# A decoder trunk whose queries and keys are projected turned and rotated there, on one core of a Trainium2 chip

## The chip, the cores and the metric

The kernel runs on one core of one Trainium2 chip. The core has a matrix engine, TensorE (PE), which multiplies a standing operand (the weights of the array, loaded ahead of each matmul) with a moving one and adds into PSUM banks of 128 partitions x 512 floats; a VectorE (DVE), a ScalarE (ACT) and a GpSimd (POOL) for the elementwise work; and DMA queues, here those that SyncE (SP) issues. Each engine works through its own instructions in order and waits for the others on semaphores. The metric is the device time of one execution in microseconds. Before the change it is 1394.22 us, the median of three runs (1393.64 to 1394.62).

## What is computed

Two layers of a decoder trunk over 512 tokens of width 1024, in float32. Each layer normalises `x`, projects it once to 2844 columns, and splits these into three groups of heads of 64 channels: forgetting attention (4 heads), sparse attention (8 query heads over 2 groups of keys and values, in a compressed, a selected and a window branch) and dilated attention (4 heads). The heads' outputs go through one output projection; then follows a gated MLP with a short convolution. The queries and keys of the sparse and the dilated heads are rotated in their first 16 channels:

```python
proj = h @ w_in
(fq, fk, fv, ff, nq, kc, vc, ks, vs, kw, vw, ng, dq, dk, dv) = jnp.split(proj, splits, axis=-1)
def partial_rope(x, cos, sin):          # half = 8, ROPE_DIM = 16 of 64 channels
    x1 = x[..., :half]
    x2 = x[..., half:ROPE_DIM]
    return jnp.concatenate([x1 * cos - x2 * sin, x2 * cos + x1 * sin, x[..., ROPE_DIM:]], axis=-1)
o_fox = fox_attention(heads(fq, 4), heads(fk, 4), heads(fv, 4), log_f)
o_nsa = nsa_attention(rope(nq, 8), rope(kc, 2), heads(vc, 2), rope(ks, 2), heads(vs, 2),
                      rope(kw, 2), heads(vw, 2), gates, ...)
o_dil = dilated_attention(rope(dq, 4), rope(dk, 4), heads(dv, 4))
x = x + rms_norm(concat(o_fox, o_nsa, o_dil) @ w_out, attn_post_norm)
x = x + rms_norm(conv_ffn(rms_norm(x, ffn_pre_norm)), ffn_post_norm)
```

With 512 tokens the selected branch has all 8 blocks selected and the window covers the whole sequence, so both are full causal attention over their own keys and values.

## The kernel before

Every operand of a large product is kept as two parts, a high and a low one, whose sum is the float32 number; a product is three matmuls (high x high, high x low, low x high). The weights come by DMA into `raw` tiles, one chunk at a time in the order of a plan; `part_weights` (L136) makes the high part on ACT (L145) and the low one on POOL (L149) or DVE (L153), chunk names in `ONPOOL` taking POOL.

The normalised tokens are kept turned, channels on partitions: `HH(k)` and `HL(k)` are the two parts of channel tile k, [128 channels, 512 tokens]. The scores need queries and keys in that layout too, 64 channels of a head on partitions and tokens along the columns; values are needed the other way, tokens on partitions.

- The projection of most columns is `proj256` (L675): 128 tokens of `HH` or `HL` stand in the array and 256 columns of weights move through it (`s_mms`, L431). The result has tokens on partitions. It takes two PSUM banks `acc` and eight steps of 12 matmuls. The names of the weight chunks are those of the columns: `kc` compressed keys and values, `ks` selected keys and values, `nq0`, `nq1` sparse queries, `kw` window keys and values, `dq`, `dk`, `dv` dilated ones; `fk`, `fv`, `fq` belong to the forgetting heads.
- `staged` (L689) says what follows for queries and keys. Per token tile `rope` (L439) rotates on DVE: three multiplies from PSUM (L442 to L444) and an add (L446) into a row tile `r`, where ACT copies the other channels (L447). Keys get each head twice side by side. Then `turn` (L709) makes four PE transposes (L712) into a bank of the group `pt`, which it shares with the attention, and `keep` parts the bank: `q_evac` (L455; ACT L459, DVE L460) makes a query's high and low part on the two halves of the partitions, `k_evac` (L464; ACT L466, DVE L467) the two parts of a key tile.
- The compressed keys and values go by `kc_evac` and `win`, with transposes at L757; the forgetting keys by `t_block` (L449), with an ACT copy that doubles them (L510) and transposes at L452. The forgetting queries (`fq_proj`) and the MLP (`up_mms`) have the weights standing and the tokens moving already.

PE's order is written by hand; that of DVE, ACT and POOL is left to a scheduler. A unit is a head, a branch and a tile of 128 queries: 16 units of the forgetting heads, 64 of the sparse ones, 16 of the dilated ones. Each slot of a loop sends several units through stages, some slots apart (`LAGS`): scores (`s<-k,q`), row maximum (L1073, DVE), exponential (ACT L1078), norm (POOL L1085), transposes (PE L1096, into `pt`), parting (ACT L1113, DVE L1118), values (`o<-ph,v`). Between the stages the loop takes steps of the other work, the pieces: `RATE` says how many per slot (1.4 in the first twelve, then 0.8); `later(d, fn)` puts a function off by d steps; and `until` takes steps at once as long as a unit's query or key isn't there (in `operands`, L1029 and L1040). `merge` mixes two pieces of a projection with one of `hidden`, the first product of the compression (`acc<-wh_w,wth`).

Of the kernel before, what the change touches and what calls it, by code (L numbers as in the profile page):

```python
# [24 lines left out]
NST = 4  # L25
# [4 lines left out]
ONPOOL = ("dv", "dq", "dk", "ks", "nq0", "kw", "kc", "nq1",  # L30
# [8 lines left out]
TT = "pt"  # L39
# [34 lines left out]
def tile_hybrid_block(  # L74
# [87 lines left out]
    for l in range(DEPTH):  # L162
# [7 lines left out]
        cols("fk", C_FK, spare=True)  # L170
        for c, (k0, k1) in enumerate(((0, 3), (3, 6), (6, 8))):
            plan.append(((l, "fv", c), [(wi[:, k0:k1, C_FV:C_FV + 260], 0, 0), (wi[:, k0:k1, C_NG:C_NG + 24], 0, 260)],
                         k1 - k0, 284, False))
        for c in range(2):
            plan.append(((l, "fq", c), [(wi[:, :, C_FQ + 128 * c:C_FQ + 128 * c + 128], 0, 0)], 8, 128, False))
        cols("kc", C_KC)
        cols("ks", C_KC + 256)
        cols("nq0", C_NQ)
        for kv, (name, c0) in enumerate((("kw", C_KW), ("nq1", C_NQ + 256))):
            for c in range(2):  # L180
                plan.append(((l, name, c), [(wi[:, 4 * c:4 * c + 4, c0:c0 + 256], 0, 0)], 4, 256, False))
# [4 lines left out]
        cols("dq", C_DQ)  # L186
        cols("dk", C_DK)
# [13 lines left out]
    def getw(*key, ahead=AHEAD, pre=None, peek=False):  # L201
        """the parts of a chunk; has those up to `ahead` after it loaded and those up to `pre` after it parted"""
# [21 lines left out]
    def table(func, after):  # L224
        """has the function's table loaded once `after` is there"""
# [20 lines left out]
    # gains of the pre norms, a channel to a partition: they are applied to the turned rows  # L246
# [8 lines left out]
    def turn_pair(half, i, l, tags, tilewise=False):  # L255
        """two token tiles of h, turned over, times the gains, in two parts"""
# [160 lines left out]
    cc = const.tile([128, NST, 16], F32, name="cc")  # L417
    ss = const.tile([128, NST, 16], F32, name="ss")
    nc.scalar.activation(ss[:, :, 8:16], ang, AF.Sin)
    nc.vector.tensor_mul(sinh, sinh, sinh)  # L420
    for o in (0, 8):
        nc.vector.tensor_scalar(cc[:, :, o:o + 8], sinh, -2.0, 1.0, op0=ALU.mult, op1=ALU.add)
    nc.vector.tensor_scalar(ss[:, :, 0:8], ss[:, :, 8:16], -1.0, None, op0=ALU.mult)

    for l in range(DEPTH):
        # ================= mixer =================
# [12 lines left out]
        def rope(dst, src, s, nh):  # L439
            t1 = small.tile([128, nh, 16], F32, tag="rope", bufs=4, name=nm("rope"))  # L440
            t2 = small.tile([128, nh, 16], F32, tag="rope", bufs=4, name=nm("rope"))
            nc.vector.tensor_mul(t1, src[:, :, 0:16], bc(cc[:, s], 1, nh))  # L442
            nc.vector.tensor_mul(t2[:, :, 0:8], src[:, :, 8:16], bc(ss[:, s, 0:8], 1, nh))
            nc.vector.tensor_mul(t2[:, :, 8:16], src[:, :, 0:8], bc(ss[:, s, 8:16], 1, nh))  # L444
# [4 lines left out]
        def t_block(tiles, c0):  # L449
            p = ps("pt")  # L450
            for s in range(NST):
                nc.tensor.transpose(p[:, 128 * s:128 * s + 128], tiles[s][:, c0:c0 + 128], ident)  # L452
            return p
# [235 lines left out]
        def staged(key, turned, dup, nh, v=None, plain=0):  # L689
# [3 lines left out]
            def evac(s, p):  # L693
# [9 lines left out]
                if v is not None:  # L703
                    if s == 0:
                        store[v] = new_v()
# [635 lines left out]
```

## Time and profile before

| | |
|---|---|
| median of three runs | 1394.22 us |
| profiled execution, span of the records | 1390.7 us |
| granted TensorE clock, mean over the span | 0.997 |
| busy: PE, DVE, ACT, POOL | 97%, 63%, 52%, 22% of the span |
| instructions: PE, DVE, ACT, POOL | 8019, 2022, 1541, 363 |

The span goes from the first to the last instruction of the profiled execution; some 3.5 us of the time lie outside it. In the rows below, a group is a line of the kernel with an engine, an operation and tiles (`out<-in`), its count, its busy time and the mean of one; behind the second bar stands the idle time of the engine just before these instructions and what ended it. In a timeline the idle time ahead of an instruction stands in brackets with its releaser. Matmuls overlap in the pipeline, so their pitch is read from their starts, not their durations. The attention of the first layer lies between 72 and 340 us, that of the second between some 740 and 1020 us.

### The profile page before, as it was taken

To read this page: it belongs to the slowest core of one execution; us is meant where nothing else is said; L and a number is where in the kernel's file an instruction comes from. 1 tells how busy PE (TensorE), PEld (TensorE's weight loads), DVE (VectorE), ACT (ScalarE), POOL (GpSimd) and SP (SyncE) were. 2 spreads that over 40 slices of the span, in tenths; PEclk is the share of its full clock that TensorE was granted. 3 is DMA by queue.
4 is the path that set the end of the run, shared out by engine and by line. 5 is a ranking of instruction groups with operands and counts; after the bars stand their busy time and mean duration, and the time that the engine had idled before them with its cause. 6 is when DMAs were issued, how large, how long until landed. Compare 5 with 4: busy or idle time off the path is not lost.

```text
span 1390.7 us, 21646 instructions
## 1 busy us (share of the span) xinstructions
PE 1343.5 (97%) x8019; PEld 1186.6 (85%) x8019; DVE 873.2 (63%) x2022; ACT 728.1 (52%) x1541; POOL 311.5 (22%) x363
## 2 busy tenths in 40 slices
PE   6999999999999999999999999999989999999997
PEld 6899999987888888888899899999878888888886
DVE  6678778678655555433464887876767555554334
ACT  6567767775443333422465677677755333333222
POOL 1363663345000000000004646633430000000000
PEclk9999999999999999999999999999999999999999
DMA  5223311132233333223323142112313333332231
GB/s 178 77 62 110 108 47 41 50 111 74 75 93 93 104 92 102 96 91 121 118 85 107 47 126 88 32 47 62 107 61 101 97 91 106 92 100 97 91 121 61
DMA packets 145521, 123.78 MB, mean 89 GB/s; under 512 B 8264, under 2 KB 135688, under 8 KB 145416
## 3 DMA queue, kind: packets, MB, share of 16 engines
q1 hardware_dynamic: 145416, 122.40, 29.1%
q8 instruction: 63, 1.03, 0.3%
q14 instruction: 42, 0.34, 0.1%
HBM read 118.19 MB, written 4.19 MB: 88 GB/s over the span
## 4 chain that ended last, share of the span: by engine, by line
PE 79%; DVE 11%; ACT 5%; issue 2%; POOL 1%; DMA 1%; SPq 0%; DVEq 0%; ACTq 0%; POOLq 0%
PE acc L114 35%; PE s L114 17%; PE pt L114 13%; PE o L114 10%; PE pt L1096 3%; DVE wt L771 1%; DVE r L1073 1%; DVE hl L267 1%; DVE x L301 1%; DVE r L446 1%; ACT r L1078 1%; ACT r L281 1%; DMA raw_fv<-in_w_in_dram 1%; DVE pl L1118 1%; ACT hh L266 0%
## 5 line engine op out<-in xcount | busy, mean ns | idle before, releaser
L153 DVE TENSOR_TENSOR wl_up<-raw_up,wh_up 128x1024 fp32r<-128x1024 f32 x78 | 95.5, 1225 | 163.2 <-ACT wh_up L145 163.2
L145 ACT ACTIVATE wh_up<-raw_up 128x1024 fp32r<-128x1024 f32 (+1 forms) x90 | 89.6, 1002 | 156.2 <-PE acc L114 68.2
L153 DVE TENSOR_TENSOR wl_wd<-raw_wd,wh_wd 128x1024 fp32r<-128x1024 f32 x42 | 51.5, 1225 | 133.6 <-ACT wh_wd L145 133.6
L1078 ACT ACTIVATE r<-r,sm 128x128 f32<-128x128 f32 x192 | 107.0, 558 | 25.6 <-DVE sm L1073 22.7
L145 ACT ACTIVATE wh_wd<-raw_wd 128x1024 fp32r<-128x1024 f32 x42 | 44.5, 1060 | 144.9 <-PE pt L114 135.6
L1085 POOL TENSOR_SCALAR r<-r,sm,gates 128x128 f32<-128x128 f32 (+3 forms) x128 | 84.1, 662 | 118.6 <-DVE sm L1083 95.9
L149 POOL TENSOR_TENSOR wl_kc<-raw_kc,wh_kc 128x512 fp32r<-128x512 f32 x8 | 11.3, 1426 | 419.7 <-ACT wh_kc L145 419.7
L114 PE MATMUL acc<-hl,wh_up 128*128 128x512 f32 (+1 forms) x272 | 102.6, 377 | 0.0
L114 PE MATMUL acc<-hh,wh_up 128*128 128x512 f32 (+1 forms) x272 | 102.6, 377 | 0.0
L114 PE MATMUL acc<-hh,wl_up 128*128 128x512 f32 (+1 forms) x272 | 102.5, 377 | 0.0
L114 PE MATMUL s<-k,q 128*128 128x512 f32 (+3 forms) x384 | 98.8, 338 | 2.3 <-DVE k L467 1.0
L1118 DVE TENSOR_TENSOR pl<-pt,ph 128x384 fp32r<-128x384 f32 x144 | 85.5, 594 | 10.2 <-ACT ph L1113 9.1
L1073 DVE CUSTOM_DVE_ANT_0 r<-s,cmask 128x128 f32<-128x128 f32 (+3 forms) x160 | 75.5, 482 | 19.3 <-PE s L114 13.8
L1113 ACT ACTIVATE ph<-pt 128x384 fp32r<-128x384 f32 x144 | 75.3, 523 | 21.3 <-PE pt L1096 19.5
L1096 PE MATMUL pt<-ident,r 128*128 128x128 f32 x480 | 77.2, 275 | 6.8 <-DVE pl L1118 3.3
L114 PE MATMUL acc<-wh_wd,gh 128*128 128x512 f32 x252 | 83.8, 389 | 0.0
L114 PE MATMUL s<-hh,wh_up 128*128 128x512 f32 (+1 forms) x224 | 80.7, 360 | 0.4 <-DVE hl L267 0.4
L114 PE MATMUL s<-hl,wh_up 128*128 128x512 f32 (+1 forms) x224 | 80.4, 359 | 0.0
L114 PE MATMUL s<-hh,wl_up 128*128 128x512 f32 (+1 forms) x224 | 80.4, 359 | 0.0
L1265 ACT ACTIVATE r<-r 128x512 f32<-128x512 f32 x44 | 27.8, 632 | 81.3 <-DVE r L1246 81.0
L114 PE MATMUL o<-ph,v 128*128 128x256 f32 (+1 forms) x288 | 69.6, 270 | 0.4 <-DVE mx L1154 0.4
L114 PE MATMUL o<-pl,v 128*128 128x256 f32 (+1 forms) x288 | 67.2, 282 | 1.9 <-DVE pl L1118 1.7
(431 smaller groups left out, 4227.7 us busy)
## 6 DMA issues: line engine op xcount, KB each, us to landing
raw_up<-in_w_up_dram SPq DMA_DIRECT2D x88, 512.0 KB, 3.8
raw_wd<-in_w_down_dram SPq DMA_DIRECT2D x44, 512.0 KB, 3.5
raw_wo<-in_w_out_dram SPq DMA_DIRECT2D x16, 512.0 KB, 3.5
x<-in_x_dram SPq DMA_DIRECT2D x8, 512.0 KB, 6.7
raw_nq<-in_w_in_dram SPq DMA_DIRECT2D x8, 512.0 KB, 3.8
raw_w<-in_cmp_w_k_dram SPq DMA_DIRECT2D x8, 512.0 KB, 3.7
raw_w<-in_cmp_w_v_dram SPq DMA_DIRECT2D x8, 512.0 KB, 3.7
raw_fk<-in_w_in_dram SPq DMA_DIRECT2D x4, 512.0 KB, 7.1
```

Of the source, the lines that this page charges most:

```text
L114: nc.tensor.matmul(o, lhsT=lhsT, rhs=rhs, start=start, stop=stop, skip_group_check=True)
L145: nc.scalar.activation(hi[:, ks], raw[:, ks], AF.Copy)
L153: nc.vector.tensor_sub(lo[:, ks], raw[:, ks], f(hi)[:, ks])
L267: nc.vector.scalar_tensor_tensor(lo, src, gain[:, k:k + 1], f(hi), op0=ALU.mult, op1=ALU.subtract)
L281: nc.scalar.activation(scr, y, AF.Square, accum_out=stats["p", s // 2][:, c:c + 1])
L1073: nc.vector.tensor_tensor_reduce(row[:, 0:n], u["S"][:, 0:n], u["mask"][:, 512 - n:512], op0=ALU.add, op1=ALU.min, scale=1.0, scalar=3.0e3 ...
L1078: nc.scalar.activation(row[:, 0:n], row[:, 0:n], AF.Exp, scale=-1.0, bias=sm_[:, 0:1], accum_out=sm_[:, 1:2])
L1085: nc.gpsimd.tensor_scalar(row[:, 0:n], row[:, 0:n], sm_[:, 2:3], g_, op0=ALU.mult, op1=ALU.mult)
L1096: nc.tensor.transpose(p[:, 128 * b:128 * b + 128], src, ident)
L1113: nc.scalar.activation(hi, src, AF.Copy)
L1118: nc.vector.tensor_sub(*u["lo"])
L1265: nc.scalar.activation(cd[0], cd[0], AF.Silu)
```

## The change

The weight chunks of all queries and keys become 128 columns of all eight channel tiles (`turned`), and the new `projT` has them standing and all 512 tokens moving: 24 matmuls of 512 columns a chunk, in four steps, into one bank. The result is turned already: two heads of 64 channels on the partitions, tokens along the columns. `rope(p)` rotates such a block whole with two tables [128, 512], `cosT` and `sinT`, that hold 1 and 0 in the channels that aren't rotated: a shuffle of partitions on DVE brings each channel's partner, DVE multiplies the block by `cosT`, POOL the shuffled one by `sinT`, and POOL adds them. The tables are built once, by 8 transposes. `q_evac` and `k_evac` read the rotated row tile; `k_evac` makes both heads of a block, each doubled over the partitions. The forgetting keys (no rotation) go from PSUM to `k_evac` straight. The values of the selected and the window branch are one chunk `sv` of 256 columns in the old layout, between `ks` and `nq0`; a unit of these heads asks for it by `until("sv")`. `dv` and `fv` stay. The transposes at L452, L712 and L757 are gone.

```diff
-        def rope(dst, src, s, nh):
...
-            for d in dst:
-                nc.vector.tensor_add(d[:, :, 0:16], t1, t2)
-                nc.scalar.activation(d[:, :, 16:64], src[:, :, 16:64], AF.Copy)
+        def t_mms(p, w, sl, first, last, ks=range(KT)):
+            hi, lo = w
+            for k in ks:
+                mm(p[:, sl], hi[:, k, :], HH(k)[:, sl], first and k == 0, False)
+                mm(p[:, sl], hi[:, k, :], HL(k)[:, sl], False, False)
+                mm(p[:, sl], lo[:, k, :], HH(k)[:, sl], False, last and k == KT - 1)
+        def rope(p):
+            w, r = rt(), rt()
+            nc.vector.stream_shuffle(w, p, PARTNER)
+            nc.vector.tensor_mul(r, p, cosT)
+            nc.gpsimd.tensor_mul(w, w, sinT)
+            nc.gpsimd.tensor_add(r, r, w)
+            return r
...
         def k_evac(p):
-            k = bt([128, 2, 512], F32R, "k")
-            nc.scalar.activation(k[:, 0, :], p, AF.Copy)
-            nc.vector.tensor_sub(k[:, 1, :], p, f(k[:, 0, :]))
-            return k
+            ks = []
+            for j in range(2):
+                k = bt([128, 2, 512], F32R, "k")
+                src = p[64 * j:64 * j + 64, :]
+                for u in (j, 1 - j):
+                    nc.scalar.activation(k[64 * u:64 * u + 64, 0, :], src, AF.Copy)
+                for u in (j, 1 - j):
+                    nc.vector.tensor_sub(k[64 * u:64 * u + 64, 1, :], src, f(k[64 * j:64 * j + 64, 0, :]))
+                ks.append(k)
+            return ks
...
-        store["fk"] = [k_evac(t_block(tl, 128 * j)) for j in range(4)]
+        store["fk"] = k_evac(pk_[0]) + k_evac(pk_[1])
...
-        def staged(key, turned, dup, nh, v=None, plain=0):
...
+        def projT(name, key=None, turn=None):
+            for c in range(sum(z[0:2] == (l, name) for z in where)):
+                w = getw(l, name, c, pre=PRE)
+                p = ps("acc")
+                for k in range(0, KT, 2):
+                    t_mms(p, w, slice(0, 512), True, True, (k, k + 1))
+                    if k == KT - 2:
+                        pieces.later(EV[0], turn[c] if turn else keep, *((p,) if turn else (p, key)))
+                    yield
+        def keep(p, key):
+            pieces.later(EV[3], keep2, rope(p), key)
+        def keep2(r, key):
+            store.setdefault(key, []).extend([q_evac(r)] if key[-1] == "q" else k_evac(r))
...
-            yield from proj256("kc", kc_evac, [(pos_turn,), (win, 0)])
-            pieces.later(3 + 4 * WGAP, win, 1)
-            yield from proj256("ks", *staged("nks", True, True, 2, "vs"))
-            yield from proj256("nq0", *staged("nq", True, False, 4))
+            pieces.later(3, pos_turn)
+            yield from projT("kc", turn=(win_k, win_v))
+            yield from projT("ks", "nks")
+            yield from proj256("sv", sv_evac, [])
+            yield from projT("nq0", "nq")
...
-            for kv, g in ((0, proj256("kw", *staged("nkw", True, True, 2, "vw"))),
-                          (1, proj256("nq1", *staged("nq", True, False, 4)))):
+            for kv, g in ((0, projT("kw", "nkw")), (1, projT("nq1", "nq"))):
...
-            yield from proj256("dq", *staged("dq", True, False, 4))
-            yield from proj256("dk", *staged("dk", True, True, 4))
+            yield from projT("dq", "dq")
+            yield from projT("dk", "dk")
```

Where this moves instructions, in the first layer. On PE, at the first score product over the window keys (`s<-k,q`), before: the end of a part of `hidden` (`acc<-..w_1_0..`) stands between the two turns of the window keys, `pt_1919` for the first head and `pt_1941` for the second:

```order
L114 MATMUL acc_1924<-wh_w_1_0_337_1889,wth_1400 128x256
L114 MATMUL acc_1924<-wl_w_1_0_338_1890,wth_1400 128x256
L712 MATMUL pt_1941<-ident,r_1777 128x128
L712 MATMUL pt_1941<-ident,r_1806 128x128
L712 MATMUL pt_1941<-ident,r_1842 128x128
L712 MATMUL pt_1941<-ident,r_1870 128x128
L114 MATMUL s_1949<-k_1946,q_1632 128x128 x2
L114 MATMUL o_1960<-ph_1701,v_298 128x256
```

On PE after, at the same product: the last matmuls of the window keys' projection (`acc_1468`) are followed by 16 of `hidden` (`acc_1510`), of which the last four stand here:

```order
L113 MATMUL acc_1510<-wh_w_0_2_274_1541,wth_949 128x256
L113 MATMUL acc_1510<-wl_w_0_2_275_1542,wth_949 128x256
L113 MATMUL acc_1510<-wh_w_0_2_274_1541,wth_949 128x256
L113 MATMUL acc_1510<-wl_w_0_2_275_1542,wth_949 128x256
L113 MATMUL s_1587<-k_1577,q_1385 128x128 x2
L113 MATMUL o_1598<-ph_1433,v_305 128x256
```

The product's place against its units is the same; what makes its key, `k_1577`, now begins at the end of `acc_1468` and not at a turn. On DVE after, around that key: the shuffle (L464) and the multiply (L465) of its block, two parts of a weight chunk of `hidden` (`wl_w`), a row maximum, and the low halves of the two keys (L488):

```order
L152 TENSOR_TENSOR wl_w_0_2_275_1542<-raw_w_0_2_270_1511,wh_w_0_2_274_1541 128x512 x2
L464 STREAM_SHUFFLE r_1555<-acc_1468 128x512
L465 TENSOR_TENSOR r_1556<-acc_1468,cosT 128x512
L152 TENSOR_TENSOR wl_w_0_3_280_1564<-raw_w_0_3_273_1539,wh_w_0_3_279_1563 128x512 x2
L1084 ISA r_1591,sm_1592<-s_1481,cmask 128x512
L1084 ISA sm_1592 128x1
L488 TENSOR_TENSOR k_1577<-r_1556,k_1577 64x512 x2
L488 TENSOR_TENSOR k_1582<-r_1556,k_1582 64x512 x2
```

On DVE before, at the low part of the same keys (L467):

```order
L153 TENSOR_TENSOR wl_w_1_1_343_1928<-raw_w_1_1_336_1887,wh_w_1_1_342_1927 128x512
L1073 ISA r_1953,sm_1954<-s_1747,cmask 128x512
L1073 ISA sm_1954 128x1
L467 TENSOR_TENSOR k_1946<-pt_1919,k_1946 128x512
L1083 RECIPROCAL sm_1954<-sm_1954 128x1
L467 TENSOR_TENSOR k_1989<-pt_1941,k_1989 128x512
```

The key's low part stood behind one weight part and one maximum and read a turned bank; it stands behind two weight parts and a maximum now, and reads a row tile that POOL finishes. On POOL the two steps of each rotation stand among the norms of the softmax rows, in one queue; ahead of those of the window keys stands the norm of a row of 384 columns. The first block of sparse queries (`nq0`) is followed on PE by three score matmuls of the last forgetting head, four transposes, 12 matmuls of the second block and then the score product that reads it.

## Rows read from the trace of the kernel before

**Rows 1.** The page: the span, the busy time of each engine, and the chain of work that ended last, by engine.

```profile
span 1390.7 us, 21646 instructions
PE 1343.5 (97%) x8019; PEld 1186.6 (85%) x8019; DVE 873.2 (63%) x2022; ACT 728.1 (52%) x1541; POOL 311.5 (22%) x363
...
PE 79%; DVE 11%; ACT 5%; issue 2%; POOL 1%; DMA 1%; SPq 0%; DVEq 0%; ACTq 0%; POOLq 0%
```

**Rows 2.** Busy time of each engine in two stretches (start:end and length in us, then busy us and instructions of each engine, the granted clock, the DMA share and GB/s): the projections beside the attention of the first layer, and a part of them.

```profile
72.00:340.00 268.00, 256.94 (x1965) 242.72 (x1964) 210.87 (x650) 188.71 (x503) 140.76 (x166) 0.99 0.25 74
82.00:105.00 23.00, 21.69 (x175) 20.80 (x174) 21.56 (x59) 15.82 (x45) 18.70 (x16) 1.00 0.17 47
```

**Rows 3.** PE's waits, by what they waited for (total us, times, longest us).

```profile
PE pt L712 <- DVE pl L1118: 4.7, 4, 2.5
PE pt L1096 <- DVE pl L1118: 3.3, 2, 1.7
...
PE s L114 <- DVE k L467: 1.0, 2, 0.5
```

**Rows 4.** The timeline of PE at the first query and the first window key of the first layer (start us, us, instruction, idle time ahead of it and its releaser).

```profile
118.18 0.60 PE L712 MATMUL pt<-ident,r 128*128 128x128 f32 x4
119.09 0.44 PE L114 MATMUL s<-k,q 128*128 128x128 f32 x2 [0.30 <-DVE q L460]
...
137.63 0.31 PE L114 MATMUL s<-k,q 128*128 128x128 f32 x1
138.42 0.33 PE L114 MATMUL s<-k,q 128*128 128x128 f32 x1 [0.48 <-DVE k L467]
```

**Rows 5.** Two pieces of the chain of waits (start us, us, what): 24 matmuls of 256 columns of a projection, and 24 of 512 columns.

```profile
372.11 5.44 PE acc L114 x24
...
755.00 2.87 PE acc L114 x24
```

**Rows 6.** The groups by line: the transposes of `turn`.

```profile
L712 PE MATMUL pt<-ident,r 128*128 128x128 f32 x112 | 17.2, 277 | 4.7 <-DVE pl L1118 4.7
```

**Rows 7.** The timeline of PE at eight transposes of the forgetting keys and at four of a turn.

```profile
45.19 1.03 PE L452 MATMUL pt<-ident,r 128*128 128x128 f32 x8
45.98 0.47 PE L114 MATMUL acc<-hh,wh_fq 128*128 128x512 f32 x1
46.30 0.39 PE L114 MATMUL acc<-hl,wh_fq 128*128 128x512 f32 x1
...
116.32 0.60 PE L712 MATMUL pt<-ident,r 128*128 128x128 f32 x4
116.67 0.36 PE L114 MATMUL acc<-wh_kw,hh 128*128 128x256 f32 x1
116.88 0.28 PE L114 MATMUL acc<-wl_kw,hh 128*128 128x256 f32 x1
```

**Rows 8.** The groups by line on DVE: the parts of the weights of `hidden`, the low parts of a query and of a key, and the rotation.

```profile
L153 DVE TENSOR_TENSOR wl_w<-raw_w,wh_w 128x512 fp32r<-128x512 f32 x32 | 23.9, 762 | 0.0
L446 DVE TENSOR_TENSOR r<-rope,rope 128x32 f32<-128x32 f32 (+1 forms) x80 | 27.6, 369 | 2.0
L460 DVE SCALAR_TENSOR_TENSOR q<-pt,q 64x512 fp32r<-64x512 f32 x24 | 16.5, 689 | 9.6 <-ACT q L459 9.2
L467 DVE TENSOR_TENSOR k<-pt,k 128x512 fp32r<-128x512 f32 x24 | 16.0, 682 | 2.0 <-ACT k L466 2.0
L442 DVE TENSOR_TENSOR rope<-acc,cc 128x64 f32<-128x64 f32 (+1 forms) x56 | 11.3, 202 | 19.9 <-PE acc L114 17.6 <-ACT r L733 1.9
L443 DVE TENSOR_TENSOR rope<-acc,ss 128x32 f32<-128x32 f32 (+1 forms) x56 | 9.6, 172 | 0.0
L444 DVE TENSOR_TENSOR rope<-acc,ss 128x32 f32<-128x32 f32 (+1 forms) x56 | 9.6, 171 | 0.0
```

**Rows 9.** The same on ACT: the copies of the rotation, and the high part of a query.

```profile
L447 ACT ACTIVATE r<-acc 128x96 f32<-128x96 f32 (+1 forms) x80 | 20.5, 291 | 26.8 <-DVE rope L444 20.3 <-PE pt L1096 3.5 <-DVE r L446 2.9
L459 ACT ACTIVATE q<-pt 64x512 fp32r<-64x512 f32 x24 | 14.2, 590 | 5.9 <-DVE q L460 4.7 <-PE pt L712 1.0
```

**Rows 10.** Two groups on DVE, by shape: windows of the compression, and a conversion.

```profile
L771 DVE TENSOR_TENSOR wt<-r,posT 64x496 f32<-64x496 f32 x8 | 13.0, 1630 | 2.4 <-ACT r L759 2.3
L590 DVE CAST r<-r 128x512 f32<-128x512 int32 x1 | 0.4, 422 | 0.0
```

**Rows 11.** Two groups on POOL, by shape: the low part of a query's weights, and the norm of a full row.

```profile
L149 POOL TENSOR_TENSOR wl_nq<-raw_nq,wh_nq 128x512 fp32r<-128x512 f32 x16 | 20.5, 1291 | 17.9 <-ACT wh_nq L145 17.7
L1085 POOL TENSOR_SCALAR r<-r,sm 128x512 f32<-128x512 f32 x16 | 11.1, 694 | 4.6 <-DVE sm L1083 4.4
```

**Rows 12.** The timeline of DVE and of POOL at the same time.

```profile
129.99 2.54 POOL L149 TENSOR_TENSOR wl_nq<-raw_nq,wh_nq 128x512 fp32r<-128x512 f32 x2 [1.27 <-ACT wh_nq L145]
...
130.01 2.57 DVE L446 TENSOR_TENSOR r<-rope,rope 128x32 f32<-128x32 f32 x2
```

**Rows 13.** Busy time and granted clock behind the stall at the post norm, in the first and in the second layer (columns as in rows 2).

```profile
330.00:338.00 8.00, 7.61 (x48) 7.30 (x49) 7.01 (x16) 6.37 (x16) 8.00 (x7) 0.79 0.42 132
1016.00:1024.00 8.00, 7.03 (x55) 6.37 (x53) 7.05 (x14) 5.43 (x14) 8.00 (x8) 1.00 0.41 133
```

**Rows 14.** The timeline of POOL at the norm of the second tile of a unit, and of PE at the transposes of the first two tiles.

```profile
72.39 0.48 POOL L1085 TENSOR_SCALAR r<-r,sm 128x256 f32<-128x256 f32 x1 [0.38 <-DVE sm L1083]
...
79.25 0.49 PE L1096 MATMUL pt<-ident,r 128*128 128x128 f32 x3
```

More of the change, by code (lines that the diff above doesn't have):

```diff
@@ L168, in cols, with turned @@
                 plan.append(((l, name, c), [(wi[:, 4 * c:4 * c + 4, c0:c0 + n], 0, 0)], 4, n, spare))
-        cols("fk", C_FK, spare=True)
+        def turned(name, *starts, spare=False):
+            for c, c0 in enumerate(starts):
+                plan.append(((l, name, c), [(wi[:, :, c0:c0 + 128], 0, 0)], 8, 128, spare))
+        turned("fk", C_FK, C_FK + 128, spare=True)
         for c, (k0, k1) in enumerate(((0, 3), (3, 6), (6, 8))):
@@ L416, in tile_hybrid_block @@
     nc.scalar.activation(sinh, ang, AF.Sin, scale=0.5)
[L417 to L419 removed]
+    ctab, stab = rt((128, NST, 128)), rt((128, NST, 128))
+    nc.gpsimd.memset(ctab, 1.0)
+    nc.gpsimd.memset(stab, 0.0)
+    nc.scalar.activation(stab[:, :, 8:16], ang, AF.Sin)
     nc.vector.tensor_mul(sinh, sinh, sinh)
[L421 to L423 removed]
+    for o in (0, 8, 64, 72):
+        nc.vector.tensor_scalar(ctab[:, :, o:o + 8], sinh, -2.0, 1.0, op0=ALU.mult, op1=ALU.add)
+    nc.vector.tensor_scalar(stab[:, :, 0:8], stab[:, :, 8:16], -1.0, None, op0=ALU.mult)
+    nc.vector.tensor_copy(stab[:, :, 64:80], stab[:, :, 0:16])
+    cosT = const.tile([128, 512], F32, name="cosT")
+    sinT = const.tile([128, 512], F32, name="sinT")
+    PARTNER = [i ^ 8 if i < 16 else i for i in range(32)]
     for l in range(DEPTH):
@@ L491, in tile_hybrid_block @@
         fv = [new_v(), new_v()]
-        tl = []
         tmode = tc.manual_schedule(engines={mybir.EngineType.PE})
@@ L497, in tile_hybrid_block @@
                 for c in range(2):
-                    for u in range(s, s + 2):
-                        s_mms(sl256(pk_, u), u, range(4 * c, 4 * c + 4), wk[c], c == 0 and u % 2 == 0,
-                              c == 1 and u % 2 == 1)
+                    t_mms(pk_[c], wk[c], slice(128 * s, 128 * s + 256), s == 0, s == 2)
             p = ps("s")[:, 0:284]
@@ L565, in fq_proj @@
         def fq_proj(c):
-            hi, lo = getw(l, "fq", c, ahead=2)
+            w = getw(l, "fq", c, ahead=2)
             p = ps("acc")
-            for k in range(KT):
-                mm(p, hi[:, k, :], HH(k), k == 0, False)
-                mm(p, hi[:, k, :], HL(k), False, False)
-                mm(p, lo[:, k, :], HH(k), False, k == KT - 1)
+            t_mms(p, w, slice(0, 512), True, True)
             store["fq"].append(q_evac(p))
@@ L1170, in cmp_values @@
             split_mix(2 + k, nc.gpsimd)
-        def up_mms(p, w, sl, first, last, ks=range(KT)):
-            hi, lo = w
-            for k in ks:
-                mm(p[:, sl], hi[:, k, :], HH(k)[:, sl], first and k == 0, False)
-                mm(p[:, sl], hi[:, k, :], HL(k)[:, sl], False, False)
-                mm(p[:, sl], lo[:, k, :], HH(k)[:, sl], False, last and k == KT - 1)
         RATE = [1.4] * 12 + [0.8] * 98
```

102 lines of the change are left out of this document (39 added, 63 removed).

## The prediction

> **What bounds the kernel now.** I read the page first: TensorE (PE) is busy 97% of the span, and the chain that ended last runs through PE for 79% of it [rows 1]. The reader should see there that time can be taken from this kernel in two ways only: fewer or shorter PE instructions, or shorter PE stalls. Next I read the stretch of the first layer in which the queries and keys are projected beside the attention: PE 256.94 of 268 us, VectorE (DVE) 210.87, ScalarE (ACT) 188.71, GpSimd (POOL) 140.76 [rows 2]. So DVE and POOL have room on average, but not everywhere: from 82 to 105 us DVE is busy 21.56 of 23 and POOL 18.70 [rows 2]. Last come PE's waits by name [rows 3]: those on work of the projections are the turn's wait for a bank (4.7 us in all) and the score product's for a fresh key (1.0); a fresh query holds it too, in single places [rows 4]. GpSimd stands in no row of this view.
>
> **PE work, removed and added.** 1152 matmuls of 256 columns become 576 of 512. In the chain 24 of the first kind take 2.87 us and 24 of the second 5.44 [rows 5]. 1152/24 x 2.87 = 137.8; 576/24 x 5.44 = 130.6: **-7.2 us**, on the path, since PE has no slack.
>
> 160 transposes go: 112 at L712 [rows 6], and by the code, over two layers, 16 in the compressed windows (L757) and 32 of the forget keys (L452). Four of them begin at 116.32 and the next matmul at 116.67, that is 0.35; its successor comes 0.21 later where the pitch of such matmuls is 0.12, so 0.09 more [rows 7]: 0.35 to 0.44 for four, and I take 0.40. 32 lots of four at L712 and L757 make 12.8. At L452 eight take 0.79, and the matmul behind the next comes 0.32 later where 0.23 is the pitch [rows 5, 7], 0.1 more; four lots of eight: 3.6. The two turned tables put 8 back, once: 0.8. Together **-15.6 us** (-14.5 to -16.6).
>
> The turn's waits for a bank of `pt`, 4.7 us, the longest of them 2.5 [rows 3], go with the turn. What is late next is the same DVE: in that stretch it is nearly full, and the attention's own transposes (L1096) already wait 3.3 us for the same `pl` [rows 3]. The change takes DVE work out: L442 to L444 are 30.5 us and L446 is 27.6 [rows 8]; shuffle and multiply, 22 blocks x 2 x 0.68 = 29.9, and the low halves of 24 keys, now 48 instructions of 0.69 for 24 of 0.68, 16.8, come in. So I keep most of it: **-3.8** (0 to -4.7).
>
> ACT loses 20.5 us at L447 and gets 24 more key instructions of 0.59, 14.2 [rows 9]; it idles 79 of the 268 us [rows 2], so nothing. The DMAs move the same bytes: nothing. The first half of each layer (forget keys without a turn) ends on the queue of q behind it; any gain there is within the 16 us above.
>
> **The new rotation, the cost that decides.** A block [128, 512] is now rotated at once: a shuffle and a multiply on DVE, a multiply and an add on POOL. No shuffle is in the trace. DVE's 128x512 pass with a conversion takes 0.42 us, its strided 64x496 pass 1.63 [rows 10]; the nearest is the key's 128x512 PSUM pass, 0.68 [rows 8], which I take for both DVE steps. POOL's steps are 128x512 with two SBUF inputs, as L149: 1.29 each; its one-input 128x512 takes 0.69 [rows 11], the lower bound. The Trainium skill ("VectorE: DVE Perf Modes", "The perf-mode tier table (the rule you actually need)") gives the shuffle its slowest mode only, some 2400 ns for 2048 elements; an estimate for 512 would be 0.6 us, and the sum would stay within 0.3 us. No run here shows it yet.
>
> By PE's order with these pitches every block but two a layer is used 13 us or more behind its last matmul, and the matmuls between cover this latency.
>
> The first query of the sparse heads: before, the score product stood right behind the second turn: turn at 118.18, 0.36 long, product at 119.09, a gap of 0.55 [rows 4]. Now there stand between its last matmul and its use 3 score matmuls and 12 of projection of 512 columns (15 x 0.227) and 4 transposes (0.44): 3.84 us. The chain is shuffle 0.68, two POOL steps 2.58, ACT 0.59, DVE 0.69 [rows 8, 9, 11] = 4.54, and up to two DVE instructions of 0.68 queued ahead: a wait of 0.7 to 2.1. I take 1.4, against 0.55: **+0.9 a layer** (0.15 to 1.55).
>
> The window keys: before, their product waited at 138.42, 0.75 later than it could have come after 137.63 [rows 4]. Now 16 matmuls of 256 columns (16 x 0.1195 = 1.91) lie between the last matmul of the block and the product. The chain is 0.68 + 2.58 + 0.59 + 2 x 0.69 = 5.23: a wait of 3.3 at least. Ahead of the key's low half DVE has two weight parts `wl_w` (0.76 each [rows 8]), and POOL a norm of about 0.69 ahead of the rotation; a row maximum stands there too, with about the time of a key's pass, 0.68: with all of them 3.3 + 1.5 + 0.7 + 0.7 = 6.2. I take 4.3, nearer the lower end because the weight parts can run while POOL works: **+3.55 a layer** (2.55 to 5.45). Behind the waiting product the whole of PE stands, and so do the units' values; nothing else can fill it, since PE's order is written out.
>
> One rule speaks against this. The row first: the adds at L446, with two SBUF inputs, take 0.37 us in the mean of 80 [rows 8], but the two at 130.01 took 2.57 us together, while POOL ran two subtractions, 2.54 us from 129.99 [rows 12]. The Trainium skill ("SBUF — State Buffer", "Who interferes with whom") says that a DVE instruction with two SBUF inputs and a GpSimd one that reads SBUF exclude each other for the whole instruction; the trace agrees. The low halves of queries and keys, which read PSUM before, read two SBUF tiles now, and POOL gets 44 more such instructions; by the rule each wl_w that meets the rotation would come only behind it and the key's wait would be at its upper end, 6.2, or 1.9 a layer on top of my sum.
>
> **The sum.** -7.2 - 15.6 - 3.8 + 2 x 0.9 + 2 x 3.55 = -17.7. The profiled span is 1390.7 [rows 1], and 3.5 us of the median of 1394.22 lie outside it: 1373.0 + 3.5 = **1376.5 us**. With all terms at their good ends: -7.2 - 16.6 - 4.7 + 0.3 + 5.1 = -23.1, 1371. At their bad ends: -7.2 - 14.5 + 0 + 3.1 + 10.9 = -7.7, 1386.5. A fall of PE's clock after a stall: a granted clock of 0.79 over the 8 us from 330 on, behind a stall for the post norm, cost 0.21 x 8 = 1.7 us; behind the same stall of the other layer it stayed at 1.00 [rows 13], so I leave it out of the sum and add one of it to the bad end. The likeliest case's own range is 1371 to 1388.
>
> **Rivals.** A, the waits hardly come: DVE's steps take the 0.42 of the conversion and POOL's the 0.69 of its norm. The query's wait vanishes (-1.1 for its 0.55 a layer), the key's is 0.84 + 1.38 + 0.59 + 1.38 - 1.91 = 2.3 (+1.5 a layer): -7.2 - 16.6 - 4.7 - 1.1 + 3.0 = -26.6, **1368** or a little under. For it: DVE's conversion is that fast [rows 10]. Against: L149 shows 1.29 for two inputs in all its groups.
>
> B, DVE and POOL hold each other up: key's and query's waits at their upper ends (+3.1 + 10.9), no bank wait gained, and each of 22 blocks holds DVE for one POOL step more, 28.4 us, of which a quarter reaches PE where DVE is full: -22.8 + 14.0 + 0 to 7.1, **1385 to 1393**. For it: 130.01 [rows 12] and the full stretch [rows 2]. Against: DVE is busy 211 of 268 us, so most such holds end in idle time.
>
> C, slower: POOL becomes the gate. Its queue is in order, and the rotations, 22 x 2.58 = 56.8 us, stand among the norms of the softmax rows (L1085), each behind a block that PE has yet to finish; a late norm holds its transposes and PE with them. The price is what is passed on: from 26.6 us (the gain without the tight places, 7.2 + 15.6 + 3.8), or 1.2 us a block, the kernel is no faster; two thirds of the 56.8 passed on would be 37.9 - 26.6 = +11.3, **1405**. For it: 18.70 of 23 us of POOL from 82 to 105 [rows 2], about where the blocks of the selected keys fall. Against: the norm of a unit ends at 72.87, its transposes come only at 79.25 [rows 14], 6.4 us of slack against 2.58; and no PE wait names POOL [rows 3].
>
> **How the numbers follow.** Forecast 0.62, A 0.13, B 0.15, C 0.08; the remaining 0.02 is that the change doesn't do what it says: the longer matmuls and the missing transposes shorten nothing on PE, and the time is that of before. A measurement of this kernel tells apart what differs by over 0.2%, 2.8 us: faster is under 1391.4, slower over 1397.0. Forecast, A and nearly all of B are faster: 0.89; same 0.05 (the rest of B, part of C, and the change that shortens nothing); slower 0.06. The range runs from 1364 (A, with the 3.3 us of L1096's own waits gone as well) to 1390 (most of B); C and a little of B and A lie outside.
>
> **What would show it.** PE instructions without L712, L757 and L452, and 24 matmuls of 512 columns in the projections at 5.44. In PE's waits the bank's row gone, and two new ones at the score product: for `q` some 1.4 and for `k` some 4.3, each twice. DVE's shuffle and multiply near 0.68, POOL's two at 1.29. Wrong if a wait for POOL's norms at L1085's transposes appears (C), if the `k` wait is 6 (B) or under 2.5 (A), or if the matmuls of 512 columns among the heads have a pitch above 0.227.

## The result and the profile after

The changed kernel takes 1413.37 us, the median of four runs (1412.11 to 1416.81), against 1394.42 for the kernel before: a ratio of 1.0135, with an interval of 1.012 to 1.015. It is slower by 19 us, where 1376.5 was forecast and 1364 to 1390 given as the range. The profiled execution is the longest of the four, 1416.81 us.

The page of the changed kernel: the span, the busy time of each engine, and the chain that ended last.

```profile
span 1415.0 us, 19975 instructions
...
PE 1337.1 (94%) x7291; PEld 1151.2 (81%) x7291; DVE 892.9 (63%) x1867; ACT 725.6 (51%) x1469; POOL 377.6 (27%) x409
...
PE 70%; DVE 12%; ACT 7%; POOL 6%; issue 3%; DMA 1%; SPq 0%; POOLq 0%; DVEq 0%; ACTq 0%
```

Against [rows 1], PE has 728 instructions fewer, but its busy time fell by 6.4 us only, its idle time rose from 47.2 us (1390.7 - 1343.5) to 77.9, and POOL holds 6% of the chain where it held 1%. The granted clock, 0.997 before, is 0.986: 1415.0 x 0.014 = 19.8 us lost for 1390.7 x 0.003 = 4.2. So the 24.3 us of the two spans are made of PE's work, some 22 less, of 15.6 more for the clock and of 30.7 more idle. From the first score product of a layer to its last the time is 11.8 us longer in the first layer and 11.7 in the second: the loss lies in the attention.

Busy time of each engine (columns of [rows 2]) over the score products of the first layer, from the first to the last, before and after; then, after, in the second stretch of [rows 2] and in two around the first window key:

```profile
67.68:300.48 232.80, 225.19 (x1803) 215.83 (x1802) 180.82 (x606) 165.75 (x453) 120.54 (x150) 1.00 0.24 70
...
68.19:312.84 244.65, 222.22 (x1479) 200.33 (x1478) 185.44 (x519) 162.67 (x413) 151.88 (x172) 0.97 0.23 66
...
82.00:105.00 23.00, 19.36 (x149) 18.14 (x147) 14.67 (x46) 14.70 (x38) 17.64 (x19) 1.00 0.21 55
130.00:140.00 10.00, 5.42 (x33) 4.58 (x31) 9.22 (x13) 7.27 (x13) 6.29 (x5) 1.00 0.23 68
140.00:150.00 10.00, 8.91 (x44) 8.51 (x45) 8.61 (x20) 6.43 (x16) 3.48 (x5) 0.66 0.56 155
```

Over the same work DVE is busy 5 us longer than before and POOL 31, but in 12 us more of time: DVE is idle for 59 of the 245 us, POOL for 93, and from 82 to 105 us, where DVE was full before, it has 8 us free (PE, which feeds it, is behind there too). By busy shares nothing is short of room; the waits say otherwise. PE's waits (as in [rows 3]):

```profile
PE s L113 <- DVE sm L1084: 8.3, 8, 1.5
...
PE s L113 <- ACT k L486: 6.7, 2, 3.4
PE acc L1004 <- DVE sm L1094: 6.7, 2, 3.4
...
PE pt L1107 <- POOL r L1096: 4.9, 4, 2.3
PE s L113 <- DVE k L488: 4.5, 2, 2.3
...
PE s L113 <- DVE q L475: 4.1, 2, 2.1
```

The wait of the turns for a bank is gone. The query's and the key's are there, and beside them three that weren't in the sum: the scores for a bank that a row maximum has yet to read (`sm`, L1084), the transposes of the compressed branch's softmax rows (L1004), and transposes for POOL's norms, which was the forecast's own sign of rival C.

At the first window key, the timelines of PE, DVE and POOL (to be held beside [rows 4]):

```profile
134.81 0.28 PE L113 MATMUL acc<-wl_w,wth 128*128 128x256 f32 x1
138.51 0.33 PE L113 MATMUL s<-k,q 128*128 128x128 f32 x1 [3.42 <-ACT k L486]
141.09 0.48 PE L113 MATMUL s<-k,q 128*128 128x128 f32 x1 [2.25 <-DVE k L488]
```
```profile
134.00 0.67 DVE L465 TENSOR_TENSOR r<-acc,cosT 128x512 f32<-128x512 f32 x1
134.59 3.10 DVE L152 TENSOR_TENSOR wl_w<-raw_w,wh_w 128x512 fp32r<-128x512 f32 x2
137.62 0.68 DVE L1084 CUSTOM_DVE_ANT_0 r<-s,cmask 128x512 f32<-128x512 f32 x1
138.22 0.08 DVE L1084 DVE_READ_ACCUMULATOR2_ANT sm<- 128x1 f32 x1
138.22 3.54 DVE L488 TENSOR_TENSOR k<-r,k 64x512 fp32r<-64x512 f32 x3
```
```profile
134.19 1.29 POOL L466 TENSOR_TENSOR r<-r,sinT 128x512 f32<-128x512 f32 x1 [3.63 <-DVE r L464]
135.55 1.59 POOL L467 TENSOR_TENSOR r<-r,r 128x512 f32<-128x512 f32 x1
137.11 3.38 POOL L148 TENSOR_TENSOR wl_nq<-raw_nq,wh_nq 128x512 fp32r<-128x512 f32 x2
```

Two weight parts take 3.10 us on DVE while POOL rotates (0.76 each in [rows 8]), and the low halves of the key run beside POOL's next weight part. PE is busy 5.42 of the 10 us up to 140, and in the 10 us after that its clock is granted at 0.66: some 3 us more. The rotation's own four steps:

```profile
L464 DVE STREAM_SHUFFLE r<-acc 128x512 f32<-128x512 f32 x22 | 16.3, 743 | 0.0
L465 DVE TENSOR_TENSOR r<-acc,cosT 128x512 f32<-128x512 f32 x22 | 14.8, 673 | 0.0
...
L467 POOL TENSOR_TENSOR r<-r,r 128x512 f32<-128x512 f32 x22 | 29.7, 1349 | 0.9
L466 POOL TENSOR_TENSOR r<-r,sinT 128x512 f32<-128x512 f32 x22 | 28.5, 1296 | 14.1 <-DVE r L464 12.4 <-PE s L113 1.0 <-PE pt L1107 0.8
```

### The profile page after: what moved, and what is told of

The parts are those of the page before. It is cut to its first block, busy times and chain, and to the rows that moved or that the text cites. A ratio compares the mean times of both kernels' runs of the same rounds, so it can differ in the third digit from the quotient of the medians.

```text
span 1415.0 us, 19975 instructions
## 1 busy us (share of the span) xinstructions
PE 1337.1 (94%) x7291; PEld 1151.2 (81%) x7291; DVE 892.9 (63%) x1867; ACT 725.6 (51%) x1469; POOL 377.6 (27%) x409
## 4 chain that ended last, share of the span: by engine, by line
PE 70%; DVE 12%; ACT 7%; POOL 6%; issue 3%; DMA 1%; SPq 0%; POOLq 0%; DVEq 0%; ACTq 0%
PE acc L113 31%; PE s L113 16%; PE pt L113 12%; PE o L113 9%; PE pt L1107 2%; DVE k L488 1%; POOL r L467 1%; DVE q L475 1%; DVE wl_w L152 1%; POOL r L466 1%; ACT r L1089 1%; POOL wt L781 1%; DVE x L308 1%; DVE hl L274 1%; DVE pl L1129 1%
## 5 line engine op out<-in xcount | busy, mean ns | idle before, releaser
L113 PE MATMUL s<-k,q 128*128 128x512 f32 (+3 forms) x384 | 100.6, 343 | 23.8 <-DVE sm L1084 8.3
L113 PEld LDWEIGHTS s<-k,q 128*128 128x128 f32 x384 | 65.0, 198 | 36.0 <-DVE sm L1084 11.8
L1107 PE MATMUL pt<-ident,r 128*128 128x128 f32 x480 | 80.1, 283 | 7.7 <-POOL r L1096 4.9
L1084 DVE CUSTOM_DVE_ANT_0 r<-s,cmask 128x128 f32<-128x128 f32 (+3 forms) x160 | 74.8, 481 | 17.4 <-PE s L113 15.3
L113 PE MATMUL o<-ph,v 128*128 128x256 f32 (+1 forms) x288 | 72.8, 279 | 0.8 <-DVE mx L1165 0.8
```

What stands on the lines that cost most here:

```text
L113: nc.tensor.matmul(o, lhsT=lhsT, rhs=rhs, start=start, stop=stop, skip_group_check=True)
L1084: nc.vector.tensor_tensor_reduce(row[:, 0:n], u["S"][:, 0:n], u["mask"][:, 512 - n:512], op0=ALU.add, op1=ALU.min, scale=1.0, scalar=3.0e3 ...
L1107: nc.tensor.transpose(p[:, 128 * b:128 * b + 128], src, ident)
```

## The experiments

Each line of a diff is against the changed kernel unless another is named; `...` stands for lines left out. The ratio is to the kernel before, run on the same chip; a ratio times 1394 gives the microseconds below.

**No rotation.**

```diff
-            pieces.later(EV[3], keep2, rope(p), key)
+            pieces.later(EV[3], keep2, p, key)
...
-                win(0, rope(p))
+                kt = rt()
+                nc.scalar.activation(kt, p, AF.Copy)
+                win(0, kt)
```

> The rotation is left out: queries and keys are parted straight from the projection's bank, and the compressed keys' block is only copied. PE's order is that of the changed kernel. Theory P (the rotation's chain through POOL, with the waits, the held queues and the clock falls behind it, is the whole loss): the gain of the layout appears, -22.8 us by the sum of PE's instructions and up to 5 more for the waits on banks, 1367 to 1376 us; granted clock 0.995 or more; no wait of PE on a query, on a key or on a norm of POOL above 1 us. Rival L (the denser order of PE itself, with one block of 512 columns in place of two half ones and the turns gone, makes the waits on score banks and on norms): they stay, 1390 us or more.

Measured 1374.83 us, ratio 0.9853 (0.9838 to 0.9868). The page:

```profile
span 1371.3 us, 19886 instructions
...
PE 1322.6 (96%) x7291; PEld 1141.0 (83%) x7291; DVE 853.8 (62%) x1801; ACT 723.7 (53%) x1471; POOL 316.3 (23%) x365
```

PE's busy time is 20.9 us under that of before, at a clock of 0.995 that costs 2.7 us more: the layout takes some 23.6 us of work from PE, where the forecast had 22.8. The longest wait on a key is 1.1 us. So rival L falls: all of the loss, some 39 us from 0.9853 to 1.0135, comes with the rotation.

**Its halves, and all of it on DVE.** In the first run POOL's two lines are dropped; in the second they go to DVE, as shown; in the third DVE also writes the product and the sum back into the PSUM bank.

```diff
-            nc.gpsimd.tensor_mul(w, w, sinT)
-            nc.gpsimd.tensor_add(r, r, w)
+            nc.vector.tensor_mul(w, w, sinT)
+            nc.vector.tensor_add(r, r, w)
```

> Only POOL's two steps of the rotation are left out (the sine's product and the sum); DVE keeps the shuffle and the product with the cosine. Theory P: nearly as without any rotation, 1368 to 1380 us. Rival D (DVE's own added work and its reads of two SBUF tiles make the loss): 1395 us or more.

> All four steps of the rotation on DVE, nothing of it on POOL. DVE gets 44 x some 0.68 = 30 us more, POOL loses 58. Theory P: waits on POOL's norms go, the key's wait shrinks to some 3 us a layer and the query's to under 1; 1378 to 1395 us. Rival D (DVE is where it is lost): 1415 us or more.

> All four steps on DVE, with the product and the sum written back to the projection's bank in PSUM, so that the low parts of queries and keys and two of the three arithmetic steps read only one SBUF tile. To be held against the run with all four steps on DVE and the sum in SBUF, 1411 us. If DVE and POOL exclude each other at two SBUF inputs for a large part of the loss: 1395 to 1405 us. If not: 1408 to 1414 us.

Without POOL's half: 1385.37, ratio 0.9930 (0.9915 to 0.9944), so DVE's half costs 10.7 us. All on DVE: 1411.29, ratio 1.0119 (1.0100 to 1.0138); in PSUM: 1411.36, ratio 1.0122 (1.0105 to 1.0139). The first two times lie between theory P (at most 1380 and 1395) and rival D (at least 1395 and 1415): neither engine alone is the gate. DVE's busy time rose by 39 us from the run without POOL's half (886.4 to 925.1), and the kernel's by 26. With the sum in PSUM DVE is busy 10 us less (914.7), and the kernel takes as long. By the third run's expectation the two engines' excluding each other is no large part of the loss there, where POOL has no step of the rotation; where POOL has two, it is tested further down.

**More distance.** The rate of the pieces; then the parting three, five and seven steps behind the rotation.

```diff
-        RATE = [1.4] * 12 + [0.8] * 98
+        RATE = [1.8] * 14 + [0.8] * 96
```
```diff
-EV = (1, 3, 1, 1)
+EV = (1, 3, 1, 5)
```

> The rotation as in the changed kernel; only the rate of the pieces is raised (1.8 a slot in the first 14 slots for 1.4 in the first 12), so that by PE's order 14 us of matmuls lie between the first query's block and its use (3.8 before) and 4.2 between the window key's and its use (1.9 before). Theory T (two late operands, and the clock falls behind their stalls, are most of the loss; the distance in PE's order cures it): the query's wait goes, the key's shrinks by 2.3, the clock fall goes: 1395 to 1402 us. Theory P in its wide form (POOL's load through the whole stretch): 1405 us or more.

> The whole rotation; a query or key is parted three steps of the pieces after its rotation is issued, not one. By PE's order 6.5 us of matmuls then lie ahead of the first query's use (3.8 before) and 4.2 ahead of the window key's (1.9), and the parts stand further back in the queues of ACT and DVE. Theory K: the engines stop standing at parts that wait for POOL, 1390 to 1405 us. Rival W: 1410 us or more.

> As before, with five steps: 9.2 and 7.4 us of matmuls ahead of the two uses. Theory K: 1380 to 1400 us. Rival W: 1410 us or more. If it is worse than with three steps, what is parted late holds something else.

> The whole rotation, parted seven steps after it is issued (one in the changed kernel; three gave 1421 us, five 1404). If distance is what helps: 1395 to 1404 us. If five was a lucky order: back to 1410 us or more.

1422.06 (ratio 1.0192), 1421.01 (1.0199), 1403.76 (1.0077) and 1417.71 (1.0161). Theory T fell: with the higher rate the first query no longer waits, and PE's waits have this in its place:

```profile
PE s L113 <- DVE sm L1084: 19.8, 6, 6.9
PE s L113 <- ACT k L486: 9.8, 2, 4.9
PE acc L1004 <- DVE pcl L1012: 6.9, 2, 3.5
```

The wait moves to whatever stands next in DVE's queue. Three, five and seven steps give no trend: with three and seven the time is that of the theory in which distance doesn't help, with five it lies between the two, so five is one order among others. Why it is 8 us better than the changed kernel is open.

**The same work, read by nobody.** The rotation's instructions stay, but queries and keys are parted from the bank of the projection. The result isn't rotated.

```diff
-            pieces.later(EV[3], keep2, rope(p), key)
+            rope(p)
+            pieces.later(EV[3], keep2, p, key)
...
-                win(0, rope(p))
+                rope(p)
+                kt = rt()
+                nc.scalar.activation(kt, p, AF.Copy)
+                win(0, kt)
```

> The rotation's four instructions a block stay, on the same engines and at the same places of the queues, but nothing reads what they make: queries and keys are parted straight from the projection's bank (so the result is not rotated). Theory K (the loss is the chain: what is parted late, what stands in the queues behind it, and the stalls of PE and the clock that follow): nearly the time without any rotation, 1375 to 1386 us. Rival W (the loss is the work itself: 44 instructions more on DVE and on POOL, and the two engines holding each other up): 1400 us or more.

1408.34, ratio 1.0102 (1.0085 to 1.0119). Theory K fell, and with it the core of the forecast: nothing waits for the rotation any more, and it costs nearly all the same. The chain as such (and the key's low halves reading SBUF and not PSUM), the changed kernel against this one, is 1.0135 - 1.0102, 4.6 us; the rest is the room that the work takes. Even the key's wait is mostly of that kind. Here the key's parts stand in the queues of ACT and DVE without a rotation to wait for, and PE still waits 4.1 us a layer for them, of 5.6 in the changed kernel:

```profile
PE s L113 <- DVE k L488: 5.4, 2, 2.7
...
PE s L113 <- ACT k L486: 2.9, 2, 1.4
```

**How POOL's time reaches PE.** Two runs on top of the last: POOL's steps on 32 columns, and memsets of the same total time in their place. By order, all four engines of the first have the same instructions at the same places as the run above; the second differs on POOL alone, but for two instructions of ACT.

```diff
-            nc.gpsimd.tensor_mul(w, w, sinT)
-            nc.gpsimd.tensor_add(r, r, w)
+            nc.gpsimd.tensor_mul(w[:, 0:32], w[:, 0:32], sinT[:, 0:32])
+            nc.gpsimd.tensor_add(r[:, 0:32], r[:, 0:32], w[:, 0:32])
```
```diff
+            for d in (w, w, r, r, r):
+                nc.gpsimd.memset(d, 0.0)
```

> As the run in which the rotation is made aside and nothing reads it (1408 us), but POOL's two steps take 32 columns in place of 512: same instructions, same waits on DVE's shuffle, same places in the queues, less of POOL's time. If it is POOL's time in its queue (norms and parts of weights behind 2.6 us a block) that costs: 1380 to 1390 us, as in the run without POOL's half (1385). If it is POOL's standing at the shuffle, or the order that the scheduler makes of everything when 44 instructions are added: 1400 us or more.

> As the run with the rotation made aside (1408 us), but POOL's two steps of 1.29 us, which read two SBUF tiles each, are replaced by five memsets of 128x512, 0.516 us each in the changed kernel's trace, 2.58 us a block, which read nothing. Theory S (POOL's reads of SBUF hold DVE's instructions with two SBUF inputs, which then come late to PE): 1383 to 1392 us, as with POOL's steps cut to 32 columns (1385). Theory Q (POOL's time in its own queue makes its norms late): 1402 us or more.

32 columns: 1385.23, ratio 0.9931 (0.9916 to 0.9946), the time without POOL's half. So it is neither the waits nor the order that make these 23.8 us, but POOL's time, of which the page has 44 us less. Memsets: 1395.77 (1388 to 1401 in ten runs), ratio 1.0003 (0.9985 to 1.0021), between the two expectations: 10.0 us for the time in POOL's queue, 13.8 more when POOL reads SBUF, each give or take some 3 us by the intervals. DVE's group of `wl_w` in the run with the whole steps, with 32 columns, and with memsets:

```profile
L152 DVE TENSOR_TENSOR wl_w<-raw_w,wh_w 128x512 fp32r<-128x512 f32 x32 | 31.4, 1005 | 1.1 <-ACT wh_w L144 0.7
```
```profile
L152 DVE TENSOR_TENSOR wl_w<-raw_w,wh_w 128x512 fp32r<-128x512 f32 x32 | 22.3, 721 | 1.1 <-ACT wh_w L144 0.7
```
```profile
L152 DVE TENSOR_TENSOR wl_w<-raw_w,wh_w 128x512 fp32r<-128x512 f32 x32 | 22.3, 723 | 1.1 <-ACT wh_w L144 0.7
```

The same 32 instructions at the same places take 721 ns or 1005, and memsets do nothing to them. This is the rule that the forecast took from the Trainium skill ("SBUF — State Buffer", "Who interferes with whom"): a DVE instruction with two SBUF inputs and a GpSimd one that reads SBUF exclude each other, one that only writes doesn't; the trace agrees. It reaches PE at the first window key: the two weight parts ahead of the key's low part take 3.11 us with the whole steps, and PE's second wait there is 2.71 us, with 32 columns 1.09:

```profile
137.41 0.47 PE L113 MATMUL s<-k,q 128*128 128x128 f32 x1 [2.71 <-DVE k L488]
```
```profile
132.82 0.48 PE L113 MATMUL s<-k,q 128*128 128x128 f32 x1 [1.09 <-DVE k L488]
```

The pages of the whole steps and of 32 columns:

```profile
span 1407.5 us, 20007 instructions
...
PE 1338.6 (95%) x7291; PEld 1155.0 (82%) x7291; DVE 889.3 (63%) x1867; ACT 723.6 (51%) x1471; POOL 375.9 (27%) x409
```
```profile
span 1383.6 us, 20005 instructions
...
PE 1327.8 (96%) x7291; PEld 1147.0 (83%) x7291; DVE 874.0 (63%) x1867; ACT 724.8 (52%) x1471; POOL 331.8 (24%) x409
```

With the same instructions in the same order, PE idles 68.9 us for 55.8, and is busy 10.8 us longer: at a clock of 0.984 for 0.991. The stalls cost 13.1 us themselves, and nearly as much again comes with the lower clock. How much the clock takes is not fixed by the program: in the ten executions with memsets its mean goes from 0.982, at 1399.53 us, to 0.996, at 1388.24.

**Moving work between DVE and POOL.** The weight parts `wl_w` to POOL; the norms to DVE.

```diff
-ONPOOL = ("sv", "dv", "dq", "dk", "ks", "nq0", "kw", "kc", "nq1",
+ONPOOL = ("w1", "sv", "dv", "dq", "dk", "ks", "nq0", "kw", "kc", "nq1",
```
```diff
-            nc.gpsimd.tensor_scalar(row[:, 0:n], row[:, 0:n], sm_[:, 2:3], g_, op0=ALU.mult, op1=ALU.mult)
+            nc.vector.tensor_scalar(row[:, 0:n], row[:, 0:n], sm_[:, 2:3], g_, op0=ALU.mult, op1=ALU.mult)
```

> The changed kernel, with the low parts of the weights of `hidden` (32 instructions of 128x512 with two SBUF inputs, 0.76 us before and 0.96 now) on POOL and not on DVE: POOL gets some 41 us, DVE loses 30, and DVE has fewer instructions that POOL can hold. Theory S: 1395 to 1408 us. Theory Q: 1418 us or more.

> The changed kernel with the norms of the softmax rows on DVE, so that nothing of the attention stands in POOL's queue behind the rotation. POOL loses 128 + 64 instructions, some 135 us; DVE gets them, at an estimated 0.2 to 0.45 us each by its conversion of 128x512 in 0.42, some 55 us. If POOL's time in front of the norms is the loss: 1385 to 1400 us. If DVE has no room for it: 1415 us or more.

1431.15 (ratio 1.0261) and 1437.88 (1.0299): either way worse. The weight parts gave POOL 40 us and took 24 from DVE, and PE's longest wait on the key rose from 3.4 to 5.6 us. Neither engine has room for the other's work, though in the changed kernel DVE is busy 63% and POOL 27% of the span.

**A part of the change.** The kernel before, with new layout and rotation for `nq1`, `dq` and `dk` (12 blocks), for `dq` and `dk` alone (8 blocks), and with the forgetting keys alone, which need no rotation.

```diff
-            yield from proj256("dq", *staged("dq", True, False, 4))
-            yield from proj256("dk", *staged("dk", True, True, 4))
+            yield from projT("dq", "dq")
+            yield from projT("dk", "dk")
```

> The kernel before, with the new layout and the new rotation for the second half of the sparse queries and for the dilated queries and keys only (12 of 22 blocks); forgetting keys, compressed, selected and window keys and the first sparse queries as before. If the loss sits in the crowded first third of the attention (80 to 160 us), these blocks keep their gain of 12/22 of 21 us or a good part: 1382 to 1392 us. If each block costs about the same wherever it stands: 1400 to 1408 us.

> The same for the dilated queries and keys alone (8 of 22 blocks), all projected behind the crowded part. If the place decides: 1384 to 1392 us. If each block costs the same: 1397 to 1402 us.

1410.77 (ratio 1.0116) and 1410.39 (1.0109; 1.0094 to 1.0124), above both expectations each time. The first scores of the run with 8 blocks come at 74.7 us for 67.7. The tables are the one work that it adds ahead of them, so their building is the likely cause; the changed kernel builds the same tables without this cost (68.2). A part of the delay is one wait for a query's low part:

```profile
68.86 0.35 PE L114 MATMUL acc<-wh_kc,hh 128*128 128x256 f32 x1 [2.94 <-DVE q L473]
```

The last scores of the layer are 13.1 us late, so four blocks behind the crowded part cost 6 us net of their gain. The crowded place, then, isn't the condition of the loss. That each block costs the same isn't shown: from the first scores of the first layer to its last it takes 5.4 us longer than before with six blocks a layer, 6.0 with four. Both kernels, like the changed one, also have six buffers for `mx` (L1160 there) where the kernel before has ten; the run without rotation has six as well and gains 20.5 us, so they aren't the loss of the change, but in these two kernels their share isn't parted from the blocks'. With the forgetting keys alone:

> The kernel before with the change's first part alone: the forgetting keys, which aren't rotated, are projected with standing weights and parted straight from their banks; no new tables, everything else as before. 32 transposes of eight at 0.89 us go, 3.6 us by the sum, and 8 copies of ACT. If PE's sum counts: 1390 to 1392 us. If the end of that half hangs on the queries' parts and not on PE, as the first scores of the changed kernel (no earlier than before) let me think: within 1.5 us of the kernel before.

1393.07, ratio 0.9986 (0.9977 to 0.9995): some 2 us faster by the ratio, and 1.5 by the medians, so it doesn't decide between its two expectations. Of the versions here with the rotation in the result it is the only one that isn't slower than the kernel before, and its gain is less than the 0.2% that the forecast called the least to be told apart.

## Why the prediction was wrong

- **PE's work: right.** 22.8 us were forecast; the page of the changed kernel gives 22.0, that without rotation 23.6. The turns' wait for a bank came out as said too: of 11.7 us that PE waited for DVE's `pl` in all, 7.3 are left, 4.4 less for the 3.8 taken. Two slips change nothing: from its own 0.35 and 0.44 the ends for the transposes are 14.0 and 16.9, and POOL's groups at L149 take 1.29 to 1.43 us, not 1.29 in all.
- **The two tight places: within their bounds, in part by luck.** The query's wait is 2.05 us a layer (0.7 to 2.1, taken 1.4). The product with the key's high part comes 3.42 us late and that with its low part 2.25 after that, 6.2 us from the end of `hidden` to the second product (3.3 to 6.2, taken 4.3): the upper end, and the sign named for rival B; the weight parts that stand ahead were held, as in the rule that was weighed and left out of the sum. But the sum reached these waits by the rotation's latency, and with nobody reading the rotation 4.1 of the key's 5.6 us are still there. The shuffle takes 0.743 us, the multiply 0.673, POOL's steps 1.30 and 1.35, near what was assumed.
- **The step that failed: "every block but two a layer is used 13 us or more behind its last matmul, and the matmuls between cover this latency".** Latency is covered, room in the queues isn't. In the run with the rotation aside nothing waits for its result, and it loses 34.7 us of the 39.3 (1.0102 - 0.9853). The forecast priced the 88 instructions, but for the two tight places, at nothing because DVE and POOL have idle time on average [rows 2]. But the attention's rows go from PE to DVE, ACT, DVE, POOL and back to PE in fixed slots, and the waits show a maximum, a parting or a norm that comes 1 or 2 us late holding PE, whose order is written out. By the ratios: DVE's half 10.7 us, POOL's time 10.0, its reads of SBUF 13.8, the chain 4.6, together 39.1 against a gain of 20.5 (0.9853).
- **The argument against rival C.** Its number, 1405, is the nearest, and what is passed on per block was the right question: POOL's 10.0 + 13.8 us are 1.1 a block, against 1.2 for its threshold and 0.9 for the gain that came (20.5/22). It was given 0.08 on the slack of one norm at the start of the attention [rows 14] and because no wait of PE names POOL [rows 3]. Neither is a measure of what 2.6 us a block more will do. And C is not the whole of it: POOL's norms hold PE 4.9 us by name, the hold on DVE is B's, and DVE's own half stands in no rival.
- **Rival B** had the hold, but passed on a quarter of 28.4 us, 7.1 at most; 13.8 came, about half.
- **The clock** was left out of the sum and given 1.7 us at the bad end; it took 15.6. It has to be counted with the stalls, though not at a fixed rate: 15.6 came with 30.7 us more idle time here, 10.8 with 13.1 between the whole steps and 32 columns.

What stays open: which instruction of DVE's queue passes on how much; whether DVE's half costs by its time or by the order that its instructions make, since no run cuts its size and keeps the order; and why five steps of distance do better than one, three or seven. What the runs show is the room, not the item.

## What to carry to other kernels

Idle time of an engine that takes part in a chain of short steps isn't room: before hiding work there, run the work with nobody reading it, which prices it apart from its latency, and once more with its size cut and all else in place. Count every stall forecast for PE with the clock that it may cost behind it, here half of the stalls' time to nearly as much again. And where two vector engines share the work, ask which of their instructions read two SBUF tiles at the same time; here moving work from POOL to DVE or back made the kernel 18 and 23 us slower still.

## What the runs showed of the hardware

- The same DVE instruction of 128x512 with two SBUF inputs takes 721 ns beside a POOL that reads little, 723 beside memsets that fill the same time, and 1005 in the mean beside two-input instructions of POOL.
- In the changed kernel PE waited 5.7 us within the 6.2 up to 141.09. From 141 to 147 us the granted clock was 0.50, the level of 1.2 GHz, with PE busy throughout, and behind that full, 2.4 GHz:

```profile
141.00:147.00 6.00, 5.91 (x26) 5.91 (x27) 4.85 (x15) 3.15 (x9) 2.23 (x3) 0.50 0.42 99
147.00:150.00 3.00, 3.00 (x20) 2.60 (x19) 2.75 (x6) 2.27 (x5) 0.76 (x2) 1.00 0.69 201
```

- In the run with 32 columns, with 13.1 us less of stalls, the mean clock over the span is 0.991 for 0.984; in ten executions of the one kernel with memsets it lies between 0.982 and 0.996.
- A shuffle of partitions of 128x512 from PSUM takes 743 ns. The Trainium skill ("VectorE: DVE Perf Modes", "The perf-mode tier table (the rule you actually need)") let one estimate 0.6; the measurement decides.
